# The v half of a spatial gating unit computed by token rows instead of by channels

## The chip, the core and the metric

The kernel runs on one core of a Trainium2 chip. The metric is device time in microseconds (us). All weights are read from device memory once per execution; activations stay in the core's on-chip memory (SBUF), and matrix products are accumulated in PSUM, which has eight banks of 512 fp32 columns in each of 128 partitions.

## What is computed

One step of an encoder layer for 320 token rows (256 of a prompt, 64 of running streams), width 2048. A normalised input is projected by `w_in`; its columns give queries, keys and values of a banded attention, and 1024 columns u and 1024 columns v of a spatial gating unit. Both mixers are normalised, concatenated, projected by `w_out`, and followed by an MLP of width 8192. What matters here is the gating:

```python
def rmsnorm(x, g):
    xf = x.astype(jnp.float32)
    y = xf * lax.rsqrt(jnp.mean(xf * xf, axis=-1, keepdims=True) + EPS)
    return (y * g.astype(jnp.float32)).astype(x.dtype)

def sgu_inputs(zs, g):
    a = jax.nn.gelu(zs)
    return a[..., :SGU_WIDTH], rmsnorm(a[..., SGU_WIDTH:], g)

def sgu_prompt(u, v, w_s, b_s):
    ...
    sp = jnp.einsum('gij,bnjgc->bnigc', ws, vb) + b_s.T[:, :, None]
    return u * sp.reshape(b, s, SGU_WIDTH)
```

So v is normalised over its 1024 channels, each of 8 channel groups is mixed over the tokens of a chunk by a matrix `ws`, and the result multiplies u. The normalised v rows of the 64 stream tokens are an output of their own (`sgu_v`).

## The kernel before, in words

**Products.** Activations are kept channels by tokens: `XH` and `XL` are 16 blocks of 128 channels by 320 tokens, the high and the low part of the normalised input, both in a reduced fp32 form (fp32r). A weight tile of 4 blocks by 256 columns (512 KB) is loaded by SP's DMA queue (`load`, line 94), split by ACT into `w_hi` (line 125) and by DVE into `w_lo` (line 126), and multiplied in three passes (line 136): `w_hi` with XH, `w_hi` with XL, `w_lo` with XH. The weights are the stationary operand (128 x 128), the activations stream as 320 columns. `products` does so for 256 output columns at a time, so one product is 16 blocks x 2 x 3 = 96 matmuls from 4 weight tiles. `w_hi` and `w_lo` have three buffers each.

**Order of the program.** First keys, values and the first quarter of the queries (line 196), with the input's loads interleaved; then the row norm of x (`rstd_rows`, line 154, and `spread`, line 165), three more products for the queries, four for v (lines 407 to 413), four for u (lines 439 to 456), 16 for `w_out`, then the MLP. Ten attention units (`attend`, line 321) are called ahead of the v products, four, three and three. A scheduler with its own timing model then decides the order of the instructions on each engine, so that attention, gating and products are interleaved; the order is fixed in the program and each engine runs it strictly.

**Scores.** A unit writes its scores by two matmuls into one PSUM tile `s_ps` of two banks (line 329), from which DVE reads four pieces (line 338); the tile has one buffer, so that the next unit's scores wait for these reads.

**The v half.** A product leaves v as 256 channels by 320 tokens. `gelu2` (line 395) scales by the row norm `rx`, and applies GELU on DVE, ACT and POOL. ACT squares and POOL adds for the norm of v (`add_square`, line 380), and POOL multiplies by the gain `g_sv` (line 413). After the fourth product the norm is taken (line 414: three small matmuls, DVE, and a power on POOL). Then 24 transposes on PE (line 422) bring v into token rows, and ACT copies them out of PSUM, scaled by the norm, into `vnat` and `vnat_s` (line 424). Eight groups follow: three matmuls with `wsT` into a bank `misc` (lines 430, 431), and DVE adds the bias `sgb` (lines 432, 435) to give `gv`, still by channels. The u products then multiply `gv` (line 453).

**After the gating.** `AH`, `AL` are the split attention output (`split`, line 175), `acc_a` the sum of its squares, added on POOL. `w_out`'s first half uses them, and its norm is `rstd_rows(acc_a)` and `spread` (line 465). Line 458 closes the pool `at`, which holds the attention's and the gating's tiles, `sgb` and `wsT` among them; the pool `wf` of the weight tiles of `w_out` and of the MLP takes its memory. So SP can issue the first load for `w_out` only when the last readers of `at` are done.

Of the kernel before, what the change touches and what calls it, by code (L numbers as in the profile page):

```python
# [8 lines left out]
F32 = mybir.dt.float32  # L9
F32R = mybir.dt.float32r  # L10
# [4 lines left out]
P = 128  # L15
T = 320
# [13 lines left out]
def hymba_step_kernel(ctx: ExitStack, tc: tile.TileContext, i, o):  # L30
# [13 lines left out]
    def misc():  # L44
        return ps_m.tile([P, 512], F32, name="misc", tag="misc")

# [59 lines left out]
    def products(w, k0, nk, jobs, rh, rl, first=None, deep=None):  # L106
# [4 lines left out]
        for a, n in chunks(nk, first is not None):  # L111
# [4 lines left out]
            for j, (c0, ps) in enumerate(jobs):  # L116
# [11 lines left out]
                tail = isinstance(ps, list) and a + n == nk  # L128
# [25 lines left out]
    def rstd_rows(sq, weight, eps, h=1):  # L154
# [6 lines left out]
        rs = sm.tile([P, 3 * h], F32, name="rs_rows", tag="rs_rows")  # L161
# [33 lines left out]
    q0_ps = ps_sc.tile([P, 2, 512], F32, name="q0_ps", tag="s_ps")  # L195
# [20 lines left out]
    nc.sync.dma_start(out=sinks, in_=i["sinks"])  # L216

# [35 lines left out]
    rx = spread(rstd_rows(ssq, inv_dm, EPS), "rx")  # L253
# [11 lines left out]
    def queries(g, q_ps):  # L265
        qg = qT[:, :, 2 * g:2 * g + 2]
        nc.vector.tensor_tensor(out=qg.rearrange("p b a t -> p a b t"),
                                in0=q_ps[:, :, 0:T].rearrange("p a (b t) -> p a b t", b=5),
                                in1=rx.rearrange("p (b t) -> p b t", b=5)[:, None].to_broadcast([P, 2, 5, 64]),
                                op=ALU.mult)  # L270
# [50 lines left out]
    def attend(unit):  # L321
# [4 lines left out]
        s_ps = ps_sc.tile([P, 2, 512], F32, name="s_ps", tag="s_ps")  # L326
        for j in range(2):
            a = 2 * (2 * kv + j)
            nc.tensor.matmul(out=s_ps[:, j, 0:2 * nk].rearrange("x (p k) -> x p k", p=2),  # L329
                             lhsT=qT[:, blk_, a:a + 2].rearrange("p a t -> p (a t)"),  # L330
                             rhs=kz[:, kv, :, k0:k0 + nk], start=True, stop=True)
# [3 lines left out]
        for p in range(2):  # L335
            for j in range(2):
                c = 2 * blk_ + p
                nc.vector.scalar_tensor_tensor(out=s[:, p, j, 0:nk], in0=s_ps[:, j, p * nk:(p + 1) * nk],
                                               scalar=rq[:, 2 * kv + j, c:c + 1],
                                               in1=bias[:, p, 2 * kv + j, b0:b0 + nk], op0=ALU.mult, op1=ALU.add)  # L340
# [64 lines left out]
    gv = blk("gv", [P, 8, T])  # L405
    acc_v = sums("acc_v")
    for g in range(4):
        attend_next((4, 3, 3, 0)[g])
        v_ps = product(w_in, 0, KT, 2304 + g * 256, xh, xl)
        gelu2(v_ps, gv[:, 2 * g:2 * g + 2])  # L410
        for a in range(2 * g, 2 * g + 2):
            add_square(acc_v, gv[:, a], a == 0)
            nc.gpsimd.tensor_scalar(out=gv[:, a], in0=gv[:, a], scalar1=g_sv[:, a:a + 1], scalar2=None, op0=ALU.mult)
    rv = rstd_rows(acc_v, inv_1k, 4 * EPS)
# [3 lines left out]
    for t, (t0, n) in enumerate(TT):  # L418
        for h in range(2):
            vps = misc()  # L420
            for a in range(4):
                nc.tensor.transpose(out=vps[0:n, a * P:(a + 1) * P], in_=gv[:, 4 * h + a, t0:t0 + n], identity=ident)  # L422
            dst = vnat[:, t] if t < 2 else vnat_s[0:HD]
            nc.scalar.activation(out=dst[:, h * 512:(h + 1) * 512], in_=vps[0:n], func=AF.Copy, scale=rv[0:n, t:t + 1])
    nc.gpsimd.dma_start(out=o["sgu_v"], in_=vnat_s[0:HD])
    for g in range(8):
        sp_ps = misc()
        cs = slice(g * P, (g + 1) * P)
        for b in range(2):
            nc.tensor.matmul(out=sp_ps[:, b * P:(b + 1) * P], lhsT=vnat[:, b, cs], rhs=wsT[:, g], start=True, stop=True)  # L430
        nc.tensor.matmul(out=sp_ps[:, 256:T], lhsT=vnat_s[:, cs], rhs=wsT[:, g, 0:HD], start=True, stop=True)  # L431
        nc.vector.tensor_tensor(out=gv[:, g, 0:256].rearrange("p (b i) -> p b i", b=2),
                                in0=sp_ps[:, 0:256].rearrange("p (b i) -> p b i", b=2),
                                in1=sgb[:, g, None, :].to_broadcast([P, 2, P]), op=ALU.add)
# [136 lines left out]
```

## Time and profile before

| | us |
|---|---|
| median of 3 runs (lowest, highest) | 1264.93 (1264.14, 1265.35) |
| the profiled execution | 1262.26 |
| its span, first to last instruction | 1259.7 |
| PE (TensorE) busy | 1252.3 |
| PE's weight loads busy | 1236.6 |
| DVE (VectorE) busy | 637.9 |
| ACT (ScalarE) busy | 489.4 |
| POOL (GpSimd) busy | 106.1 |

The profile is of one execution. A row of a group gives a line, an engine, the tiles written and read, the shape, the count, the busy time, the mean of one and the idle time ahead of them. A matmul's recorded duration overlaps that of its neighbours, so the time that a matmul costs is read from the chain of work that ended last, where a row gives a start, a length and a count of instructions in a row. An fp32 matmul is recorded as two instructions, an fp32r matmul or a transpose as one.

### The profile page before, as it was taken

What the parts mean: (1) busy time and instruction counts of PE and PEld (TensorE: products, weight loads), DVE (VectorE), ACT (ScalarE), POOL (GpSimd) and SP (SyncE); (2) the same over time, 40 slices, a digit from 0 to 9 for tenths busy, and PEclk for the clock granted to TensorE, in tenths of its full rate; (3) what the DMA queues carried; (4) which work ended last, traced back from release to release, by engine and by line L of the source; (5) the groups of instructions that cost most, each with busy time, mean ns of one, the idle gap of its engine ahead of it and who ended that gap; (6) DMA issues with size and microseconds to landing.
All of it is one profiled execution on the core that took longest, in us unless ns stands there. A gap on an engine that the chain in (4) does not pass through costs nothing.

```text
span 1259.7 us, 20182 instructions
## 1 busy us (share of the span) xinstructions
PE 1252.3 (99%) x8519; PEld 1236.6 (98%) x8519; DVE 637.9 (51%) x731; ACT 489.4 (39%) x636; POOL 106.1 (8%) x104
## 2 busy tenths in 40 slices
PE   8999999999999999999999999999999999999998
PEld 7998889999999999999999999999999999999998
DVE  7547857756864444444444444444444334444443
ACT  7335546533543342223333333343333333343221
POOL 2213452400310000000000000000000000000000
PEclk9999999999999999999999999999999999999999
DMA  8643233644454444445544444455444444444550
GB/s 281 191 136 116 85 109 119 216 148 137 151 149 148 152 149 149 149 147 150 150 150 151 150 151 151 151 151 151 150 151 150 146 148 149 148 153 160 169 169 32
DMA packets 186426, 187.77 MB, mean 149 GB/s; under 512 B 6464, under 2 KB 185856, under 8 KB 186336
## 3 DMA queue, kind: packets, MB, share of 16 engines
q1 hardware_dynamic: 185696, 185.43, 47.2%
q8 instruction: 66, 1.08, 0.4%
q0 software_dynamic: 496, 1.03, 0.3%
q14 instruction: 24, 0.20, 0.0%
q10 hardware_dynamic: 144, 0.03, 0.0%
HBM read 182.91 MB, written 3.32 MB: 148 GB/s over the span
## 4 chain that ended last, share of the span: by engine, by line
PE 98%; DMA 0%; SPq 0%; ACT 0%; issue 0%; DVE 0%
PE acc L136 93%; PE misc L136 1%; PE q_ps L136 1%; PE s_ps L329 1%; PE misc L374 1%; PE misc L365 1%; DMA xT<-in_xT 0%; SPq L99 0%; PE misc L275 0%; PE misc L430 0%; PE misc L158 0%; PE misc L422 0%; PE misc L169 0%; ACT XH L178 0%; PE misc L431 0%; ACT w_hi L125 0%
## 5 line engine op out<-in xcount | busy, mean ns | idle before, releaser
L126 DVE TENSOR_TENSOR w_lo<-w_raw,w_hi 128x1024 fp32r<-128x1024 f32 x332 | 413.6, 1246 | 460.6 <-ACT w_hi L125 451.2
L125 ACT ACTIVATE w_hi<-w_raw 128x1024 fp32r<-128x1024 f32 x332 | 351.9, 1060 | 708.0 <-PE acc L136 674.6
L136 PE MATMUL acc<-H2H,w_hi 128*128 128x320 f32 x1024 | 316.6, 309 | 0.0
L136 PE MATMUL acc<-H2L,w_hi 128*128 128x320 f32 x1024 | 316.4, 309 | 0.0
L136 PE MATMUL acc<-H2H,w_lo 128*128 128x320 f32 x1024 | 316.4, 309 | 0.0
L136 PE MATMUL acc<-FH,w_hi 128*128 128x320 f32 x992 | 306.5, 309 | 0.0
L136 PE MATMUL acc<-FL,w_hi 128*128 128x320 f32 x992 | 306.5, 309 | 0.0
L136 PE MATMUL acc<-FH,w_lo 128*128 128x320 f32 x992 | 306.5, 309 | 0.0
L136 PEld LDWEIGHTS acc<-H2L,w_hi 128*128 128x128 f32 x1024 | 192.2, 188 | 0.0
L136 PEld LDWEIGHTS acc<-H2H,w_hi 128*128 128x128 f32 x1024 | 192.2, 188 | 0.0
L136 PEld LDWEIGHTS acc<-H2H,w_lo 128*128 128x128 f32 x1024 | 192.2, 188 | 0.0
L136 PEld LDWEIGHTS acc<-FH,w_hi 128*128 128x128 f32 x992 | 186.2, 188 | 0.0
L136 PEld LDWEIGHTS acc<-FL,w_hi 128*128 128x128 f32 x992 | 186.2, 188 | 0.0
L136 PEld LDWEIGHTS acc<-FH,w_lo 128*128 128x128 f32 x992 | 186.2, 188 | 0.0
L136 PE MATMUL acc<-XH,w_hi 128*128 128x320 f32 x384 | 117.2, 316 | 1.2 <-ACT w_hi L125 1.1
L136 PE MATMUL acc<-XH,w_lo 128*128 128x320 f32 x384 | 116.8, 315 | 0.0
L136 PE MATMUL acc<-XL,w_hi 128*128 128x320 f32 x384 | 116.6, 314 | 0.0
L136 PEld LDWEIGHTS acc<-XH,w_hi 128*128 128x128 f32 x384 | 71.2, 189 | 4.7 <-ACT w_hi L125 2.2
L136 PEld LDWEIGHTS acc<-XL,w_hi 128*128 128x128 f32 x384 | 71.4, 189 | 2.4 <-issue 1.9
L136 PEld LDWEIGHTS acc<-XH,w_lo 128*128 128x128 f32 x384 | 71.1, 188 | 2.2 <-issue 1.5
L488 DVE SCALAR_TENSOR_TENSOR tf<-acc,r 128x640 f32<-128x640 f32 x32 | 26.4, 825 | 42.7 <-PE acc L136 42.7
L502 DVE TENSOR_TENSOR xT<-xT,acc 128x640 f32<-128x640 f32 x31 | 25.5, 821 | 41.8 <-PE acc L136 41.8
(176 smaller groups left out, 1016.9 us busy)
## 6 DMA issues: line engine op xcount, KB each, us to landing
w_raw<-in_w_up SPq DMA_DIRECT2D x128, 512.0 KB
w_raw<-in_w_down SPq DMA_DIRECT2D x128, 512.0 KB
w_raw<-in_w_in SPq DMA_DIRECT2D x44, 512.0 KB
w_raw<-in_w_out SPq DMA_DIRECT2D x32, 512.0 KB
w_first<-in_w_in SPq DMA_DIRECT2D x6, 512.0 KB
out_yT<-xT SPq DMA_DIRECT2D x7, 320.0 KB
xT<-in_xT SPq DMA_DIRECT2D x3, 640.0 KB
w_first<-in_w_in SPq DMA_DIRECT2D x8, 128.0 KB
```

The lines of the kernel that those rows point to most:

```text
L125: high = pin(nc.scalar.activation(out=hi[:, :n], in_=raw[:, :n], func=AF.Copy))
L126: low = pin(nc.vector.tensor_tensor(out=lo[:, :n], in0=raw[:, :n], in1=hi[:, :n].bitcast(F32), op=ALU.subtract))
L136: mm = nc.tensor.matmul(out=out, lhsT=w_[:, k, g * P:(g + 1) * P], rhs=r_(kk), start=(kk == 0 and x == 0), stop=(kk == nk - 1 and x == 2))
L329: nc.tensor.matmul(out=s_ps[:, j, 0:2 * nk].rearrange("x (p k) -> x p k", p=2), lhsT=qT[:, blk_, a:a + 2].rearrange("p a t -> p (a t)"), r ...
L365: nc.tensor.transpose(out=pt_ps[0:n, (2 * p + j) * P:(2 * p + j + 1) * P], in_=s[:, p, j, c:c + n], identity=ident)
L374: nc.tensor.matmul(out=o_ps[p * HD:(p + 1) * HD, 0:256], lhsT=v[0:n, kv], rhs=pt[0:n, p * 256:(p + 1) * 256], start=(x == 0), stop=(x == l ...
L488: nc.vector.scalar_tensor_tensor(out=t, in0=ps[:, :, 0:T], scalar=0.0, in1=r2[:, None, :].to_broadcast([P, 2, T]), op0=ALU.max, op1=ALU.mult)
L502: nc.vector.tensor_tensor(out=xT[:, a:a + n], in0=xT[:, a:a + n], in1=p, op=ALU.add)
```

## The change

For the v half the operands change places. Blocks of `XH` and `XL` with 128 tokens are stationary, and weight tiles of 2 blocks by 512 columns stream (`rows_product`). For each block there are three passes for each of the two prompt halves; for the 64 stream tokens a new tile `XS`, filled by POOL, holds XH and XL side by side as 128 stationary columns, so two passes (`w_hi`, `w_lo`) do. The two halves of its result are added afterwards through ACT and DVE (`low`). v so has two products of 16 x 8 = 128 matmuls of 512 columns, in place of four of 96 matmuls of 320 columns; the number of weight tiles, loads and splits is the same (16 of 512 KB).

v now lies in token rows. `gelu2_rows` takes the row norm of x as a scalar per partition (`rx_rows`, kept from `rstd_rows`), and ACT's last square also sums along the row (`acc_v`), so that the norm needs neither matmuls nor POOL's additions, and the 24 transposes go. ACT scales `vnat` and `vnat_s` in place. The gain moves behind the mixing (a scalar per channel in DVE's bias step); for the output `sgu_v` it is applied on POOL from a row copy of the gain, which a DMA writes at the start to device memory (`g_dram`, 1024 single values) and two DMAs read back later.

The v half needs a third PSUM bank for the stream rows, `v_s`. It takes one of the two banks of the scores: a unit's two score matmuls now use the single bank `s_ps` in turn, and the second waits for DVE's reads of the first. The first query product is written to these two banks separately. Attention units are called six and four ahead of the two products.

```diff
-    q0_ps = ps_sc.tile([P, 2, 512], F32, name="q0_ps", tag="s_ps")
+    q0_ps = [single("s_ps"), single("v_s")]
...
+    g_dram = dram.tile([8, P], F32, name="g_dram")
+    nc.gpsimd.dma_start(out=g_dram.rearrange("a p -> p a"), in_=g_sv)
...
-        s_ps = ps_sc.tile([P, 2, 512], F32, name="s_ps", tag="s_ps")
...
+        for j in range(2):
+            a = 2 * (2 * kv + j)
+            s_ps = single("s_ps")
+            nc.tensor.matmul(out=s_ps[:, 0:2 * nk].rearrange("x (p k) -> x p k", p=2),
+                             lhsT=qT[:, blk_, a:a + 2].rearrange("p a t -> p (a t)"),
+                             rhs=kz[:, kv, :, k0:k0 + nk], start=True, stop=True)
+            for p in range(2):
...
-    for g in range(4):
-        attend_next((4, 3, 3, 0)[g])
-        v_ps = product(w_in, 0, KT, 2304 + g * 256, xh, xl)
-        gelu2(v_ps, gv[:, 2 * g:2 * g + 2])
-        for a in range(2 * g, 2 * g + 2):
-            add_square(acc_v, gv[:, a], a == 0)
-            nc.gpsimd.tensor_scalar(out=gv[:, a], in0=gv[:, a], scalar1=g_sv[:, a:a + 1], scalar2=None, op0=ALU.mult)
-    rv = rstd_rows(acc_v, inv_1k, 4 * EPS)
...
+    XS = blk("XS", [P, KT, P], F32R)
+    nc.gpsimd.tensor_copy(out=XS[:, :, 0:HD], in_=XH[:, :, 256:T])
+    nc.gpsimd.tensor_copy(out=XS[:, :, HD:P], in_=XL[:, :, 256:T])
+
+    def rows_product(c0, ps, ps_s):
+        wv = w_in.rearrange("(kt p) n -> p kt n", p=P)
+        for a in range(0, KT, 2):
+            raw = wp.tile([P, 2, 512], F32, name="w_raw", tag="w_raw")
...
+            passes = [(t, k, x, w) for t in range(2) for k in range(2) for x, w in ((0, hi), (1, hi), (0, lo))]
+            passes += [(2, k, None, w) for k in range(2) for w in (hi, lo)]
...
+                st = XS[:, a + k] if t == 2 else (XH, XL)[x][:, a + k, t * P:(t + 1) * P]
...
+                nc.tensor.matmul(out=ps_s if t == 2 else ps[:, t], lhsT=st, rhs=w[:, k], start=(a == 0 and n == 1),
+                                 stop=(a == KT - 2 and n == (4 if t == 2 else 6)))
...
-            for a in range(4):
-                nc.tensor.transpose(out=vps[0:n, a * P:(a + 1) * P], in_=gv[:, 4 * h + a, t0:t0 + n], identity=ident)
...
+    for g in range(2):
+        attend_next((6, 4)[g])
+        cs = slice(g * 512, (g + 1) * 512)
+        v_ps, vs_ps = acc_tile(), single("v_s")
+        rows_product(2304 + g * 512, v_ps, vs_ps)
+        low = sm.tile([P, 512], F32, name="low", tag="w2", bufs=4)[0:HD]
+        nc.scalar.activation(out=low, in_=vs_ps[HD:P], func=AF.Copy)
+        nc.vector.tensor_tensor(out=low, in0=vs_ps[0:HD], in1=low, op=ALU.add)
...
+    for t in range(2):
+        nc.scalar.activation(out=vnat[:, t], in_=vnat[:, t], func=AF.Copy, scale=rv[:, t:t + 1])
+    nc.scalar.activation(out=vnat_s[0:HD], in_=vnat_s[0:HD], func=AF.Copy, scale=rv[0:HD, 2:3])
```

The scheduler orders the whole program anew. The place where this shows most is the passage from the u products to `w_out`. On PE before, from the last mixing matmuls of the gating (wsT) over the last u products (XH, XL) to the first products of `w_out` (AH, AL) and the norm sum of the attention (acc_a):

```order
L430 MATMUL misc<-wsT,vnat 128x128
L431 MATMUL misc<-wsT,vnat_s 128x64
L136 MATMUL acc<-XH,w_hi 128x320
...
L136 MATMUL acc<-XH,w_lo 128x320
L136 MATMUL acc<-AH,w_hi 128x320 [waits Activation_49]
L136 MATMUL acc<-AL,w_hi 128x320
L136 MATMUL acc<-AH,w_lo 128x320 [waits DVE_49]
...
L158 MATMUL misc<-inv_1k,acc_a 128x1 [waits Pool_49]
L158 MATMUL misc<-inv_1k,acc_a 128x1 x2
```

Here 138 u matmuls stand between the last mixing and the first AH, and 42 product matmuls between the norm's sums (line 158) and the matmuls that spread it (line 169). On PE now, at the same place:

```order
L490 MATMUL misc<-wsT,vnat_s 128x64
L139 MATMUL acc<-XL,w_hi 128x320
...
L139 MATMUL acc<-XH,w_lo 128x320
L161 MATMUL misc<-inv_1k,acc_a 128x1 [waits DVE_49,PE_49,Pool_49]
L161 MATMUL misc<-inv_1k,acc_a 128x1 x2
L139 MATMUL acc<-AH,w_hi 128x320 [waits Activation_49]
L139 MATMUL acc<-AL,w_hi 128x320
L172 MATMUL misc<-ident,rs_rows 128x128 [waits PE_49,Pool_49]
L172 MATMUL misc<-ident,rs_rows 128x128
L172 MATMUL misc<-ident,rs_rows 128x64
L139 MATMUL acc<-AH,w_lo 128x320 [waits DVE_49]
```

The last mixing matmuls have moved to 35 u matmuls ahead of the first AH, and two product matmuls are left between the norm's sums and the spread. On DVE before, from the last reader of `sgb` (gv<-misc,sgb) over the first `w_lo` of `w_out` (the row that also waits for DMASW3) to the norm's row r_rows:

```order
L432 TENSOR_TENSOR gv<-misc,sgb 128x256 [waits PE_49]
L435 TENSOR_TENSOR gv<-misc,sgb 128x64
...
L126 TENSOR_TENSOR w_lo<-w_raw,w_hi 128x1024 [waits DMASW3_49,DMAHW6_49,PE_49,Activation_49]
L179 SCALAR_TENSOR_TENSOR SL<-gv,cols,SH 128x320 [waits DVE_49,Activation_49]
L179 SCALAR_TENSOR_TENSOR SL<-gv,cols,SH 128x320 [waits Activation_49]
L126 TENSOR_TENSOR w_lo<-w_raw,w_hi 128x1024 [waits DMAHW7_49,PE_49,Activation_49]
L397 TENSOR_TENSOR z<-acc,rx 128x640 [waits PE_49]
L126 TENSOR_TENSOR w_lo<-w_raw,w_hi 128x1024 [waits DMAHW0_49,Activation_49]
L400 TENSOR_SCALAR gc<-gc 128x640 [waits Activation_49,Pool_49]
L160 TENSOR_SCALAR r_rows<-misc 128x3 [waits PE_49]
```

Three weight tiles of `w_out` are split ahead of r_rows. On DVE now, the same stretch:

```order
L415 SCALAR_TENSOR_TENSOR gu<-gc,z 128x640 [waits Activation_49]
L514 SCALAR_TENSOR_TENSOR gv<-gv,gu 128x640 [waits DVE_49]
L182 SCALAR_TENSOR_TENSOR SL<-gv,cols,SH 128x320 [waits PE_49]
L182 SCALAR_TENSOR_TENSOR SL<-gv,cols,SH 128x320 x2
L492 SCALAR_TENSOR_TENSOR gv<-misc,cols,sgb 128x256 [waits PE_49]
L495 SCALAR_TENSOR_TENSOR gv<-misc,cols,sgb 128x64
L182 SCALAR_TENSOR_TENSOR SL<-gv,cols,SH 128x320
L182 SCALAR_TENSOR_TENSOR SL<-gv,cols,SH 128x320 [waits DVE_49,Activation_49]
L182 SCALAR_TENSOR_TENSOR SL<-gv,cols,SH 128x320 [waits Activation_49]
L409 TENSOR_TENSOR z<-acc,rx 128x640 [waits PE_49]
L163 TENSOR_SCALAR r_rows<-misc 128x3 [waits PE_49]
L129 TENSOR_TENSOR w_lo<-w_raw,w_hi 128x1024 [waits DMAHW6_49,Activation_49]
```

The last reader of `sgb` (line 495) now stands four rows ahead of r_rows, and the first `w_lo` of `w_out` behind r_rows and behind z of the last u product.

More of the change, by code (lines that the diff above doesn't have):

```diff
@@ L334, in attend @@
             nc.gpsimd.memset(s[:, :, :, nk:P], 0.0)
-        for p in range(2):
-            for j in range(2):
+        for j in range(2):
[5 more added lines that the diff above has]
+            for p in range(2):
                 c = 2 * blk_ + p
-                nc.vector.scalar_tensor_tensor(out=s[:, p, j, 0:nk], in0=s_ps[:, j, p * nk:(p + 1) * nk],
+                nc.vector.scalar_tensor_tensor(out=s[:, p, j, 0:nk], in0=s_ps[:, p * nk:(p + 1) * nk],
                                                scalar=rq[:, 2 * kv + j, c:c + 1],
```

82 lines of the change are left out of this document (57 added, 25 removed).

## The prediction, on record before the run

> **What bounds the kernel now.** I read the page first, then the chain of work that ended last, then PE's waits and the groups of the other engines.
>
> ```profile
> span 1259.7 us, 20182 instructions
> PE 1252.3 (99%) x8519; PEld 1236.6 (98%) x8519; DVE 637.9 (51%) x731; ACT 489.4 (39%) x636; POOL 106.1 (8%) x104
> ```
>
> PE is busy for all but 7.4 us of the span; the profiled execution took 1262.26 us, 2.56 more than its span and 2.67 less than the median of 1264.93. I work out a difference to the profile and add it to the median. A measurement of this kernel can tell about 0.2%, 2.5 us, from no change.
>
> ```profile
> PE acc L136 <- ACT w_hi L125: 1.1, 1, 1.1
> 15.82 2.61 PE acc L136 x16
> 99.22 0.86 PE s_ps L329 x4
> 127.27 1.29 PE s_ps L329 x4
> 186.62 0.56 PE misc L158 x6
> 195.75 0.87 PE misc L422 x8
> 204.50 0.50 PE misc L430 x4
> 218.33 21.75 PE acc L136 x148
> 240.08 0.56 PE misc L158 x6
> 367.98 874.34 PE acc L136 x5961
> ```
>
> The first row, of PE's waits, is from the start of the program: later than that PE waits for nobody, the whole gating included. The others are rows of the chain (start, length, what). So two things count: how long PE's own instructions take, and whether the new order makes PE wait. A product matmul of 320 columns costs 874.34 / 5961 = 0.1467 us.
>
> **The matmuls of v.** Before: 384 x 0.1467 = 56.3 us. After: 256 matmuls of 512 columns, a size that the trace does not show. Its nearest rows are the fp32 score matmuls: 256 columns cost 0.86 / 4 = 0.215 us an instruction, 384 columns 1.29 / 4 = 0.3225, each instruction streaming its columns twice. The slope is 0.1075 / 256 = 0.00042 us per streamed column, and almost nothing is left at zero. At that slope 320 columns are 0.134 us, so an fp32r product carries 0.013 us on top. If this is fixed per matmul, 512 columns cost 0.215 + 0.013 = 0.228 us, or 58.3 us in all: 2.0 us more than before. If it vanishes for longer streams, 0.215 x 256 = 55.0, 1.3 less; if it grows with the columns, 0.1467 x 1.6 x 256 = 60.1, 3.8 more. I take the fixed case. Weight loading is not what makes it up: the norm's sums (line 158) stream one column and cost 0.56 / 6 = 0.093 us with their load, well below 0.1467.
>
> The Trainium skill, in "TensorE: Matmul & The Clock Gate", section "Back-to-back issue gap", gives a warm gap of columns / 2.4 + 2.5 ns. For 320 columns that is 136 ns, which the 147 ns of the trace contradict; for 512 it is 216 ns, an estimate by which v's matmuls would come to 55.2 us. That is the case of the vanishing extra, a rival below.
>
> ```profile
> L422 PE MATMUL misc<-ident,gv 128*128 128x128 f32 x16 | 2.4, 274 | 0.0
> L422 PE MATMUL misc<-ident,gv 128*64 128x128 f32 x8 | 1.2, 273 | 0.0
> ```
>
> **The transposes and the norm.** 24 transposes go, at 0.87 / 8 = 0.109 us: 2.6 us. The three sums of `acc_v` go, one 0.56 row. Both lie on PE, which has no idle time there: 3.2 us less. The mixing and the score matmuls stay the same in number.
>
> **Elementwise work.** POOL loses eight gains and seven additions and gets six products of 512 columns, two of the output's gain, the two `XS` copies and three more DMA issues.
>
> ```profile
> L401 POOL TENSOR_TENSOR gc<-gc,z 128x640 f32<-128x640 f32 x8 | 12.5, 1567 | 13.2 <-DVE gc L400 12.3 <-DVE nm L346 0.5 <-DVE r_rows L160 0.4
> L413 POOL TENSOR_SCALAR gv<-gv,cols 128x320 f32<-128x320 f32 x8 | 11.0, 1379 | 3.3 <-ACT acc_v L382 3.3
> L386 POOL TENSOR_TENSOR acc_v<-acc_v,sq 128x320 f32<-128x320 f32 x7 | 8.2, 1177 | 12.3 <-ACT sq L385 7.7 <-DVE den L356 4.6
> L126 DVE TENSOR_TENSOR w_lo<-w_raw,w_hi 128x1024 fp32r<-128x1024 f32 x88 | 114.6, 1303 | 64.9 <-ACT w_hi L125 63.0 <-PE misc L365 0.6
> L397 DVE TENSOR_TENSOR z<-acc,rx 128x640 f32<-128x640 f32 x8 | 6.5, 818 | 4.7 <-PE acc L136 4.7
> L399 ACT ACTIVATE gc<-z 128x640 f32<-128x640 f32 x8 | 5.8, 731 | 1.0 <-DVE z L397 0.9
> ```
>
> That is some 10 us less for POOL. GELU now runs over 6 x 512 columns instead of 4 x 640, a fifth more, and `low` is new: about 3 us more on DVE and on ACT (0.8 and 0.7 us per 640 columns).
>
> ```profile
> 120.00:140.00 20.00, 20.00 (x124) 16.68 (x123) 18.45 (x35) 10.68 (x28) 8.05 (x6) 1.00 0.36 107
> 200.00:220.00 20.00, 20.00 (x151) 20.00 (x150) 14.52 (x26) 11.56 (x21) 6.18 (x7) 1.00 0.39 119
> ```
>
> In these two stretches of the attention and the gating DVE (third time) is busy for 18.45 and 14.52 of 20 us, ACT (fourth) for 11 to 12, and PE is never idle; so I cost this at nothing. Without that cover it would be those 3 us. The second score matmul of a unit waits for two reads by DVE; the order puts some 20 instructions of PE, over 2 us, between the two, so I cost this at nothing too. What is queued behind that wait is the next product on PE, so a miss would cost PE directly.
>
> **The passage from u to `w_out`.** Here I expect a new wait. The split scores draw the attention out: its last output matmul now has 125 u matmuls behind it, where it had 319. The gating follows it, and only its last reader of `sgb` releases the memory in which `w_out`'s weights land.
>
> ```profile
> 221.53 0.21 DVE L435 TENSOR_TENSOR gv<-misc,sgb 128x64 f32<-128x64 f32 x1
> ...
> 221.90 1.47 SPq L99 DMA_DIRECT2D w_raw<-in_w_out  x3
> ...
> 33.12 0.44 SPq L99 DMA_DIRECT2D w_raw<-in_w_in  x1
> ...
> 37.12 1.06 ACT L125 ACTIVATE w_hi<-w_raw 128x1024 fp32r<-128x1024 f32 x1 [5.33 <-DMA w_raw<-in_w_in]
> ```
>
> The first two rows show this release: the last reader ends at 221.74, SP issues at 221.90, and u then runs to about 238.6, so 17 us cover the load. The last two show a load that ACT waited for: 4.0 us from issue to use, then 1.06 us on ACT. So the first `w_hi` comes some 5.2 us after the release.
>
> Now place the release. From the last attention output PE has 125 x 0.1467 = 18.3 us of u and eight mixing groups (0.50 for line 430, some 0.1 for line 431): 23 us. DVE has, by the order, from there to the last reader of `sgb`: three `w_lo` (3.9), eight bias steps (5.0), eight `AL` (4.3), three gv<-gv,gu (2.5), one each of z, gc, gu (2.4), three `SL` (1.6 to 3.2).
>
> ```profile
> L432 DVE TENSOR_TENSOR gv<-misc,sgb 128x256 f32<-128x256 f32 x8 | 3.3, 417 | 2.3 <-PE misc L431 2.2
> L435 DVE TENSOR_TENSOR gv<-misc,sgb 128x64 f32<-128x64 f32 x8 | 1.7, 211 | 0.0
> L179 DVE SCALAR_TENSOR_TENSOR AL<-ao,cols,AH 128x320 fp32r<-128x320 f32 x8 | 4.2, 542 | 0.0
> L179 DVE SCALAR_TENSOR_TENSOR SL<-gv,cols,SH 128x320 fp32r<-128x320 f32 x8 | 8.2, 1060 | 0.0
> L453 DVE SCALAR_TENSOR_TENSOR gv<-gv,gu 128x640 f32<-128x640 f32 x4 | 3.3, 822 | 0.1
> ```
>
> That is 19.7 to 21.3 us in a row, and it starts some 0.8 us after the last attention output; so the release comes 1 to 3 us before u ends (4 if some of it runs ahead), the first `w_hi` 1 to 4 us after it, and `w_lo`, 1.3 us, 2.5 to 5.5 us after.
>
> A second chain sets a floor. DVE runs z of the last product (0.82) and r_rows ahead of that `w_lo`, and only two product matmuls stand between the sums and the spread.
>
> ```profile
> 241.19 0.14 DVE L160 TENSOR_SCALAR r_rows<-misc 128x3 f32<-128x3 f32 x1
> 242.87 0.87 POOL L162 TENSOR_TENSOR rs_rows<-r_rows,nhalf 128x3 f32<-128x3 f32 x1
> ```
>
> From u's end: 0.2 to z, 0.82, 0.14, 0.1, 0.87, so the spread starts at 2.2 and ends at 2.8. Before, these steps lay under 42 matmuls. PE's own work there is 0.56 + 0.3 + 0.6 = 1.5 us. So PE idles 1.3 us at the least and 4 at the most. I take 2.6. POOL's last additions of `acc_a` (1.2 us each, as for `acc_v`) can hold the sums as well; by the same count they end within 1 us of u's end, inside this range.
>
> **The start.** `g_dram` is written by 1024 single values while the input loads fill the queues, and PE waits for them:
>
> ```profile
> 6.41 6.16 DMA xT<-in_xT
> 0.00:20.00 20.00, 15.93 (x82) 13.90 (x83) 11.89 (x31) 13.62 (x26) 6.08 (x18) 1.00 0.89 279
> q1 hardware_dynamic: 185696, 185.43, 47.2%
> ```
>
> A packet of this queue takes 0.472 x 16 x 1259.7 / 185696 = 0.051 us of an engine, nearly all of 1 KB. 1024 of them on 16 engines are 3.3 us, the upper bound; the lower is nothing, since 4 KB are 0.1% of what these 20 us move and 11% of the engines' time is free. I take 0.6, nearer to nothing. The Trainium skill, "DMA: Bandwidth & Descriptors", section "Rules for kernel authors", says that a strided last dimension becomes one descriptor per element, and so speaks against this write. No row here shows such a DMA; the full 3.3 us would add 2.7 to my sum.
>
> **Sum.** 2.0 - 3.2 + 2.6 + 0.6 = 2.0 us more. 1264.9 + 2.0 = 1266.9, that is 0.16% more, within what counts as the same.
>
> **The rivals.**
> *The extra of a product vanishes at 512 columns, and the new wait is at its floor* (0.19): -1.3 - 3.2 + 1.3 + 0.1 = -3.1, 1261.8. For it: weights are reloaded for every matmul, and a longer stream hides more of that. Against it: the 0.093 us with load.
> *The release comes late* (0.20): DVE's chain is at its slow end, with POOL beside it (`SL` took 1.06 us against 0.54 for the same shape in `AL`, `w_lo` 1.30 in the mean), or the attention ends later still. From the point where the release falls less than 2.5 us before u's end, every us late is one on the total. At 3 us later than in my sum: +5.0, 1269.9, slower. Against it: from 200 to 220 us DVE was idle for 5.5 of 20 us, and could run ahead.
> *The extra grows with the columns* (0.15): 3.8 - 3.2 + 2.6 + 0.6 = 3.8, 1268.7, slower. For it: 0.1467 is 1.1 times 0.134; against it: the fp32 rows show no such slope.
> *The forecast* has the rest, 0.46.
>
> **How the numbers follow.** The forecast's own terms move by about 1.5 either way; 0.08 of its 0.46 falls beyond +2.5 us and 0.05 below -2.5. Faster: 0.15 of the first rival, 0.05 here, 0.20. Slower: 0.20, 0.11 of the last rival, 0.08 here: 0.39. The same: 0.41. The range takes in the first rival's value and most of the late release, 1261.8 to 1271.0; what it leaves out is a release later than that, or the full 3.3 us at the start on top of a slow matmul.
>
> **What would show it.** The chain should show v's matmuls at 0.215, 0.228 or 0.235 us each. PE's waits should show one new wait of 1.3 to 4 us ahead of the spread or of the first `AH`, ended by POOL, ACT or DVE, with the first `w_out` load issued under 3 us before u ends. Then the start: the first long run of products began at 15.8 us and should begin up to 1 us later. I am wrong if PE idles within the v half or at the scores, which I cost at nothing, or if the load for `w_out` lands in time and PE does not wait at all; then the sum is -0.6 and the kernel stays the same or gets faster.

## The result, and the profile after

The changed kernel takes 1274.62 us (median of 4 runs, 1274.46 to 1275.65), the kernel before 1264.57 beside it (1264.14 to 1265.35): a ratio of 1.0081, 95% interval 1.0063 to 1.0098. It is slower by 10 us, and outside the predicted range of 1261.8 to 1271.0.

The first lines of the page of the changed kernel, and PE's waits in its trace (engine, tile and line, what was waited for: us in total, times, longest):

```profile
span 1272.7 us, 19881 instructions
...
PE 1256.1 (99%) x8361; PEld 1228.6 (97%) x8361; DVE 645.1 (51%) x741; ACT 491.7 (39%) x643; POOL 97.9 (8%) x99
```

```profile
PE acc L139 <- ACT w_hi L128: 8.5, 5, 4.7
PE s_ps L139 <- ACT w_hi L128: 2.5, 1, 2.5
...
PE misc L161 <- POOL acc_a L398: 0.8, 1, 0.8
```

The span grew by 13.0 us, PE's idle time from 7.4 to 16.6. The other 3.8 us are *busy* time, although the change takes work away from PE. Waits for weights are 11 us, where before they were 2.6. Rows of the chain that ended last (start, length, what) say where:

```profile
6.41 13.48 DMA xT<-in_xT
...
23.13 3.83 PE acc L139 x16
...
95.45 2.75 PE acc L439 x12
98.20 0.91 PE v_s L439 x4
...
240.39 1.38 DVE gv L514
...
244.63 1.06 POOL acc_a L398
245.69 3.46 DMA w_raw<-in_w_out
...
249.26 1.07 ACT w_hi L128
...
250.37 0.56 PE acc L139 x2
250.93 0.85 PE misc L172 x6
```

The input load that took 6.16 us before takes 13.48, and the first long run of products begins at 23.13, not at 15.82. v's matmuls of 512 columns cost 2.75 / 12 = 0.229 us. At the passage from u to `w_out` the first load is issued at 245.69, when u is already at its last matmul, and PE has the first `AH` product at 250.37.

The windows of both kernels add what the chain does not say. The columns are: stretch, length, busy time of PE, PEld, DVE, ACT, POOL; then the granted clock, the DMA share, GB/s. The changed kernel:

```profile
10.00:15.00 5.00, 1.64 (x12) 1.38 (x10) 0.89 (x2) 0.56 (x1) 0.00 (x0) 1.00 0.62 36
15.00:20.00 5.00, 1.97 (x6) 1.57 (x6) 0.43 (x1) 0.51 (x2) 0.00 (x0) 0.56 0.83 244
20.00:25.00 5.00, 3.83 (x13) 3.43 (x14) 4.16 (x7) 4.91 (x9) 0.00 (x0) 0.50 1.09 352
25.00:30.00 5.00, 5.00 (x33) 5.00 (x32) 4.86 (x9) 5.00 (x9) 0.00 (x0) 0.91 1.09 353
240.00:260.00 20.00, 16.50 (x105) 16.11 (x104) 16.96 (x22) 9.67 (x16) 12.21 (x11) 0.91 0.69 224
```

The same stretches before:

```profile
10.00:15.00 5.00, 3.15 (x20) 2.61 (x18) 2.05 (x6) 2.41 (x6) 0.00 (x0) 1.00 1.03 345
15.00:20.00 5.00, 4.18 (x28) 4.18 (x29) 4.56 (x6) 4.98 (x8) 0.00 (x0) 1.00 1.09 357
20.00:25.00 5.00, 5.00 (x34) 4.38 (x32) 5.00 (x9) 5.00 (x9) 0.00 (x0) 1.00 1.10 358
...
240.00:260.00 20.00, 20.00 (x141) 20.00 (x140) 14.22 (x17) 7.81 (x11) 5.12 (x5) 1.00 0.43 141
```

Two things are to be seen. From 10 to 15 us the input loads move 36 GB/s and not 345. And the granted clock, 1.00 everywhere before, falls to 0.50 after each of the two idle stretches: matmuls behind a wait run at half speed for some us. That is the busy time that the sum had no term for.

A table by stage makes this exact. Read from the starts of PE's product matmuls in the trace: *start* is up to the 101st product, *middle* from there to the last u product (queries, attention, v, mixing, u), *passage* from there to the 101st `w_out` product; the rest is within 0.1 us the same in both.

| us in the profile | start | middle | passage | span |
|---|---|---|---|---|
| before | 24.27 | 214.04 | 16.15 | 1259.7 |
| changed | 32.81 | 212.91 | 21.70 | 1272.7 |
| difference | +8.54 | -1.13 | +5.55 | +13.0 |

The spans differ by 13.0, the times of the two profiled executions by 12.2 (1274.46 and 1262.26) and the medians by 10.05: the profiled execution of before lies 2.3 us below its median and had one of the quick starts that are told of under the clock.

### The profile page after: what moved, and what is told of

Its sections match the earlier page's. It is cut to its first block, busy times and chain, and to the rows that moved or that the text cites. A ratio compares the mean times of both kernels' runs of the same rounds, so it can differ in the third digit from the quotient of the medians.

```text
span 1272.7 us, 19881 instructions
## 1 busy us (share of the span) xinstructions
PE 1256.1 (99%) x8361; PEld 1228.6 (97%) x8361; DVE 645.1 (51%) x741; ACT 491.7 (39%) x643; POOL 97.9 (8%) x99
## 3 DMA queue, kind: packets, MB, share of 16 engines
q8 instruction: 65, 1.06, 0.3%
## 4 chain that ended last, share of the span: by engine, by line
PE 97%; DMA 1%; DVE 1%; ACT 0%; SPq 0%; issue 0%; POOL 0%; ACTq 0%
PE acc L139 87%; PE acc L439 3%; PE v_s L439 1%; PE misc L139 1%; DMA xT<-in_xT 1%; PE s_ps L345 1%; PE misc L386 1%; PE misc L377 1%; PE s_ps L139 0%; PE v_s L139 0%; SPq L102 0%; PE misc L288 0%; DMA w_raw<-in_w_out 0%; PE misc L172 0%; ACT w_hi L128 0%; PE misc L489 0%
## 5 line engine op out<-in xcount | busy, mean ns | idle before, releaser
L129 DVE TENSOR_TENSOR w_lo<-w_raw,w_hi 128x1024 fp32r<-128x1024 f32 x316 | 394.7, 1249 | 447.3 <-ACT w_hi L128 438.5
L128 ACT ACTIVATE w_hi<-w_raw 128x1024 fp32r<-128x1024 f32 x316 | 334.8, 1060 | 686.6 <-PE acc L139 652.9
L139 PE MATMUL acc<-XH,w_hi 128*128 128x320 f32 x256 | 78.0, 322 | 5.9 <-ACT w_hi L128 5.9
L139 PE MATMUL acc<-XH,w_lo 128*128 128x320 f32 x256 | 77.6, 319 | 0.0
L139 PE MATMUL acc<-XL,w_hi 128*128 128x320 f32 x256 | 77.0, 317 | 0.0
L139 PEld LDWEIGHTS acc<-XH,w_hi 128*128 128x128 f32 x256 | 48.2, 194 | 9.0 <-ACT w_hi L128 7.9
L139 PEld LDWEIGHTS acc<-XL,w_hi 128*128 128x128 f32 x256 | 47.9, 192 | 2.1 <-issue 1.9
L139 PEld LDWEIGHTS acc<-XH,w_lo 128*128 128x128 f32 x256 | 47.4, 189 | 1.6 <-issue 0.8
```

The costliest lines, as they stand in the source:

```text
L128: high = pin(nc.scalar.activation(out=hi[:, :n], in_=raw[:, :n], func=AF.Copy))
L129: low = pin(nc.vector.tensor_tensor(out=lo[:, :n], in0=raw[:, :n], in1=hi[:, :n].bitcast(F32), op=ALU.subtract))
L139: mm = nc.tensor.matmul(out=out, lhsT=w_[:, k, g * P:(g + 1) * P], rhs=r_(kk), start=(kk == 0 and x == 0), stop=(kk == nk - 1 and x == 2))
```

## The experiments

Theory W: the write of the gain alone holds up the start. Theory P: the late release of the gating's memory makes the passage. Theory G: an idle stretch of PE costs more than itself, through the clock that is granted behind it. The rival V: the v half by rows costs the time. Each kernel is "before" or "changed" with one edit. Where the median of before is named, it is that of the same chip: 1264.4 to 1264.7.

**The write alone**, put into the kernel before (`b_write`), then as 128 pieces of 32 bytes (`b_write32`), then as 1024 pieces of 32 bytes (`b_write1k32`):

```diff
+    g_dram = dram.tile([8, P], F32, name="g_dram")
+    nc.gpsimd.dma_start(out=g_dram.rearrange("a p -> p a"), in_=g_sv)
```
```diff
+    g_dram = dram.tile([P, 8], F32, name="g_dram")
+    nc.gpsimd.dma_start(out=g_dram, in_=g_sv)
```
```diff
+    x_dram = dram.tile([8, P, 8], F32, name="x_dram")
+    nc.gpsimd.dma_start(out=x_dram.rearrange("a p r -> p a r"), in_=xT[:, 0, 0:64].rearrange("p (a r) -> p a r", a=8))
```

Expected of `b_write`: 

> The kernel before with only the write of the 1024 single gain values added, at the place where the changed kernel has it; nothing reads it. Theory W (the write alone holds up the input loads): 1264.6 + 8.5 = 1273 us (1272 to 1274.5), the first long run of products from about 23 us as in the changed kernel, not from 15.8. Rival V (the v half by rows, or the new order of the start, is what costs the time; the write only stands beside it): 1264 to 1266, the run from 15.8 to 16.8 us.

Expected of `b_write32`: 

> The kernel before with the same 4 KB written at the same place, but as 128 pieces of 32 bytes (the gain laid out by partition) instead of 1024 of 4 bytes. If the write costs by its pieces (W1): an eighth of 8.5, so 1265 to 1266. If any small write from this queue at this place holds up the loads (W2): about 1273 again. By rival V: 1264 to 1266, as for the first kernel.

Expected of `b_write1k32`: 

> The kernel before with 1024 pieces again at the same place, but of 32 bytes each (64 columns of the first input tile, eight at a time), 32 KB in all; nothing reads them. Theory N (the number of pieces holds up the loads): 1269 to 1271 us as with 1024 pieces of 4 bytes. Theory B (pieces of 4 bytes are what is dear, whatever their number): 1263 to 1265.5, as with 128 pieces of 32 bytes.

Measured: 1269.74 (ratio 1.0052, interval 1.0038 to 1.0067), 1262.70 (0.9991, 0.9981 to 1.0000) and 1261.97 (0.9987, 0.9978 to 0.9997). The row of each in the list of DMA issues (queue, number, KB, median us from issue to landing), in this order:

```profile
g_dram<-cols POOLq DMA_DIRECT2D x1, 4.0 KB, 10.1
```
```profile
g_dram<-cols POOLq DMA_DIRECT2D x1, 4.0 KB, 3.8
```
```profile
x_dram<-xT POOLq DMA_DIRECT2D x1, 32.0 KB, 4.2
```

All three are issued at 4.4 us. 1024 pieces of 32 bytes, eight times the data, land in 4.2 us, and the start is 24.51 us, against 24.27 before; 1024 pieces of 4 bytes take 10.1, and meanwhile the loads nearly stand. In the windows of `b_write`, which has no other change:

```profile
10.00:15.00 5.00, 3.44 (x14) 3.04 (x14) 0.85 (x2) 0.98 (x3) 0.00 (x0) 0.71 0.66 52
15.00:20.00 5.00, 2.37 (x7) 1.97 (x8) 1.62 (x4) 2.05 (x6) 0.00 (x0) 0.50 0.97 306
```

Its start is 32.08 us, middle and passage are those of before to 0.01 us. So theory W holds, and rival V falls for the start; not the number of pieces is dear, since as many of 32 bytes cost nothing. One rival is left untried: the 4-byte pieces also lie side by side in memory, eight of them in the 32 bytes that are one piece of `b_write1k32`, and 4-byte pieces far apart may cost less. My numbers for the median missed: I took 8.5 from the profiles, it is 5.4. The two 32-byte kernels came out 1.7 and 2.7 us *below* before, and below what I expected of them; the interval of the first touches 1, that of the second ends just under it. Part of it is the clock: four of the ten runs of each have a mean clock of 1.000, against 7 of 86 of before. Why their starts keep it more often is not shown.

**The changed kernel without the write**, the gain row read from an added input row of 1024 contiguous values (`a_input`), and with the same write later (`a_late`):

```diff
-    g_dram = dram.tile([8, P], F32, name="g_dram")
-    nc.gpsimd.dma_start(out=g_dram.rearrange("a p -> p a"), in_=g_sv)
...
-        nc.gpsimd.dma_start(out=sv, in_=g_dram.rearrange("a p -> (a p)")[None, g * 512:(g + 1) * 512]
-                            .to_broadcast([HD, 512]))
+        nc.gpsimd.dma_start(out=sv, in_=i["sgu_g"][:, g * 512:(g + 1) * 512].to_broadcast([HD, 512]))
```
```diff
-    g_dram = dram.tile([8, P], F32, name="g_dram")
-    nc.gpsimd.dma_start(out=g_dram.rearrange("a p -> p a"), in_=g_sv)
...
     for g in range(1, 4):
         queries(g, product(w_in, 0, KT, g * 256, xh, xl))
+    g_late = sm.tile([P, 8], F32, name="g_late", tag="g_late")
+    nc.vector.scalar_tensor_tensor(out=g_late, in0=rq[:, 2, 0:8], scalar=0.0, in1=g_sv, op0=ALU.mult, op1=ALU.add)
+    g_dram = dram.tile([8, P], F32, name="g_dram")
+    nc.gpsimd.dma_start(out=g_dram.rearrange("a p -> p a"), in_=g_late)
```

Expected of `a_input`: 

> The changed kernel, its gain row read from an input row of 1024 contiguous values, without the write. Theory W: 1274.6 - 8.5 = 1266 us (1265 to 1267), the first long run of products back at 15.8 us, and PE's idle 3.5 to 4 us at the passage from u to w_out still there. Rival V: 1273 to 1275.

Expected of `a_late`: 

> The changed kernel with the same 1024 single values written later, once the third group of queries is normed (at about 75 us), while the weight loads run up to three buffers ahead of PE. Theory W with the loads' lead as cover: the loads are held up again, but three buffers are some 10 us of products, so 1266 to 1268. If the lead is shorter than the hold-up: up to 1274, with a wait of PE for w_hi of some us behind the write. Rival V: 1273 to 1275 without such a wait.

Measured: 1268.79 (1.0037, 1.0024 to 1.0049) and 1270.07 (1.0048, 1.0031 to 1.0065). `a_late`'s write takes as long as ever, and its windows behind the write, the last two lines, show the loads slowed again:

```profile
g_dram<-g_late POOLq DMA_DIRECT2D x1, 4.0 KB, 10.2
...
85.00:90.00 5.00, 5.00 (x36) 5.00 (x35) 1.62 (x2) 1.06 (x1) 0.00 (x0) 1.00 0.25 25
90.00:95.00 5.00, 5.00 (x25) 4.18 (x24) 2.34 (x4) 1.75 (x2) 0.00 (x0) 1.00 0.50 39
```

But PE has no wait behind it, and the middle is 212.98 us against 212.91: three buffers of lead cover it. In the profiles its passage is 0.9 us longer than that of `a_input` (22.62 against 21.73; the clock stayed low for 6.8 us there instead of 3.4); whether that is its 1.3 us in the median is open, since the runs of `a_input` alone lie between 1265.17 and 1270.85. Both medians were forecast too low, for one reason: I took off the 8.5 us of the profiles for the write, and between the medians it is 5.8 (1274.62 less 1268.79). What is left over the kernel before is the passage. In the windows of `a_input`:

```profile
220.00:240.00 20.00, 17.54 (x128) 17.19 (x126) 18.93 (x28) 10.56 (x24) 16.19 (x14) 1.00 0.14 45
240.00:260.00 20.00, 18.94 (x119) 18.85 (x120) 15.46 (x17) 10.35 (x13) 5.07 (x4) 0.91 0.92 298
```

PE is idle for 2.46 + 1.06 = 3.5 us, and the second stretch loses 0.09 x 20 = 1.8 us to the clock. 1264.4 of before, less 1.1 in the middle, and 5.6 more in the passage are 1268.9, against the measured 1268.8; with runs that lie 5.7 us apart, so close an agreement is in part luck.

**The passage.** `a_wp` and the three below are `a_input` with a further edit. The first `w_out` product takes its weights through the pool of `w_in`'s, which waits for no release; in `a_wp2` the norm is also asked for behind that product; in `a_wp4` the first two products do so (without `a_wp2`'s edit), and `a_wp3` is that with the fill at the start that is told of below:

```diff
-            ps = product(i["w_out"], 8 * half, 8, g * 256, lambda k: hi[:, k], lambda k: lo[:, k], wf)
+            ps = product(i["w_out"], 8 * half, 8, g * 256, lambda k: hi[:, k], lambda k: lo[:, k],
+                         wf if half or g else None)          # a_wp4, a_wp3: wf if half or g > 1 else None
```
```diff
-        rm = spread(rstd_rows(acc, inv_1k, EPS), f"rm{half}")
         for g in range(8):
             ps = product(...)
+            if g == 0:
+                rm = spread(rstd_rows(acc, inv_1k, EPS), f"rm{half}")
```

Expected of `a_wp`: 

> The changed kernel without the write (gain row from an input), and the weights of the first w_out product land in the buffers of w_in, which need no release of the gating's memory. Theory P (that release makes the passage idle) with theory G (more than some 3 us of idle PE also halve the granted clock for the next us): PE idles under 1.5 us at the passage, the clock stays at 1.0 there, and the time is 1268.8 - 2.5 - 1.5 to 3 = 1263.5 to 1265 us. Rival S (the sums of acc_a on POOL and the spread set the passage, not the load): 1267.5 to 1269, PE idle still 3 us or more.

Expected of `a_wp2`: 

> The kernel with the first w_out product from the buffers of w_in, and the norm of the attention half asked for behind that product and not ahead of it. What PE still waits for there is 0.6 us for POOL's acc_a and 1.3 us for POOL's rs_rows; theory P with the floor of the prediction (the norm's chain): both go, 1265.7 - 1.9 = 1264 us (1263 to 1265). Rival: the waits move to the next product or to DVE, 1265 to 1266.5.

Expected of `a_wp3`: 

> The changed kernel without the write, the first two w_out products from the buffers of w_in, and the fill at the start (6 and 4 identity matmuls). With one product from there the chain of the norm (r_rows on DVE) still stood behind a w_lo that waited for the released memory; with two it should not: the passage costs 0.5 to 1 us over that of the kernel before, the middle is 1.1 shorter, the start 2.2: 1264.6 + 0.8 - 1.1 - 2.2 = 1262.1 us (1261.3 to 1263.3). Rival (POOL or DVE hold the norm up all the same): 1263.5 to 1265.

Expected of `a_wp4`: 

> The same without the fill at the start, so that the start is that of the kernel before: 1264.6 + 0.8 - 1.1 = 1264.3 us (1263.5 to 1265.5). Rival: 1265.5 to 1267.

| | us (median) | ratio to before | middle | passage |
|---|---|---|---|---|
| `a_input` | 1268.79 | 1.0037 (1.0024 to 1.0049) | 212.91 | 21.73 |
| `a_wp` | 1265.70 | 1.0003 (0.9993 to 1.0013) | 212.91 | 18.58 |
| `a_wp2` | 1266.38 | 1.0016 (1.0007 to 1.0026) | 212.92 | 19.40 |
| `a_wp4` | 1263.80 | 0.9995 (0.9985 to 1.0005) | 212.92 | 17.12 |
| `a_wp3` | 1262.06 | 0.9984 (0.9975 to 0.9993) | 212.91 | 17.12 |

In `a_wp2` the norm's sums of the second half of `w_out`, some 0.65 us, fall into the passage and are missing in the rest; beside the others its passage counts as 18.75.

`a_wp` shows theory P: without the wait for the release the passage is 3.15 us shorter, and the clock stays at 1.00 there. PE's idle time there, 1.9 us, and the median are a little above what I had forecast (under 1.5, and 1263.5 to 1265). What is left, in PE's waits:

```profile
PE misc L172 <- POOL rs_rows L165: 1.3, 1, 1.3
...
PE misc L161 <- POOL acc_a L396: 0.6, 1, 0.6
```

is the floor of the prediction, the norm's chain, and POOL's last addition ahead of it. What holds the norm up stands in the order of time of DVE (in brackets: idle before, and who ended it):

```profile
245.51 1.23 DVE L129 TENSOR_TENSOR w_lo<-w_raw,w_hi 128x1024 fp32r<-128x1024 f32 x1 [1.37 <-ACT w_hi L128]
246.65 0.15 DVE L163 TENSOR_SCALAR r_rows<-misc 128x3 f32<-128x3 f32 x1
```

`r_rows`, 0.15 us long, could run from 242, when its sums are done, and stands behind a `w_lo` whose weights do wait for the release. Asking for the norm later only moved this: in `a_wp2` the wait for `acc_a` is gone, but `r_rows` ran behind `gu` and `gv` of the last group, and the wait for `rs_rows` grew by as much. The edit was a miss.

```profile
PE misc L172 <- POOL rs_rows L165: 1.9, 1, 1.9
```

With two products clear of the release (`a_wp4`, `a_wp3`) the wait for `rs_rows` is gone, and of `a_wp3`'s passage this is left:

```profile
PE misc L165 <- POOL acc_a L400: 0.6, 1, 0.6
```

**The scores' one bank alone** (`b_one`): the kernel before with `single("s_ps")` per score matmul and the first queries in two single banks, as in the diff of the change.

Expected: 

> The kernel before with the scores, and the first queries, in single PSUM banks as in the changed kernel; v's half and all else as before. My forecast of nothing for this part: 1264.4 us, 1 either way, PE waiting nowhere in the scores; the attention ends later in the v half but u's 17 us still cover the load of w_out. Rival (the one bank holds up the attention so far that the passage gets late by itself): 1266 to 1270, with PE idle between u and w_out.

Measured: 1265.13 (1.0004, 0.9995 to 1.0013). Middle 214.12, passage 17.04: PE waits nowhere in the scores. The rows of the order give u products behind the last attention output: 319 before, 242 here, 125 in the changed kernel. So the bank draws the attention out, by some two thirds as far in matmuls of u as the rest of the change does; which part of that rest it is (the work on DVE and ACT, or the order of v's products) was not tried. 0.6 us of the 0.9 more in the passage are a wait for POOL's `acc_a`.

**The clock.** Identity matmuls that compute nothing used, put into a wait: at the passage of `a_input`, 28 (`a_warm`) and 11 (`a_warm2`); at the start of the kernel before, 10 and 4 ahead of the fifth tile's two products (`b_warm`), and 6 ahead of the fourth tile's second and 4 ahead of the fifth's first (`b_warm2`):

```diff
+    keep_ps = misc()
+    for _ in range(28):                                      # a_warm2: 11
+        with tc.issue_after(steps[-1][2]):
+            nc.tensor.matmul(out=keep_ps[:, 0:P], lhsT=ident, rhs=ident, start=True, stop=True)
```
```diff
                 load(raw[:, :n], wv[:, k0 + a:k0 + a + n, c0:c0 + 256])
+                if first is not None:
+                    for _ in range({(3, 1): 6, (4, 0): 4}.get((a, j), 0)):     # b_warm: {(4, 0): 10, (4, 1): 4}
+                        tc.keep_in_program_order(nc.tensor.matmul(out=warm_ps[:, 0:P], lhsT=ident, rhs=ident,
+                                                                  start=True, stop=True))
```

Expected of `a_warm`: 

> The changed kernel without the write, and 28 matmuls of the identity (about 0.11 us each, 3 us) in the idle stretch between u and w_out; they compute nothing that is used. The wait itself stays. Theory G: the granted clock stays at 1.0 over the passage and the products behind it run at full speed: 1268.8 - 1.5 to 3 = 1266 to 1267.3 us. Rival (the lower clock does not come from PE's idle stretch, or costs nothing): 1268.5 to 1269.5, the clock falling there as before.

Expected of `a_warm2`: 

> The changed kernel without the write, with 11 identity matmuls (2.45 us) between u and w_out, so that they fit into the wait of some 3.5 us and do not outlast it, as the 28 did (6.2 us). Theory G: the load still comes late, the clock stays at 1.0 there, 1268.8 - 1.5 to 3 = 1266 to 1267.3 us. Rival: 1268.5 to 1269.5, the clock falls at the passage all the same.

Expected of `b_warm`: 

> The kernel before with 14 matmuls of the identity (1.5 us in all) in the waits for the first input loads, 10 ahead of the fifth tile's first products and 4 ahead of its second. Theory G: the runs of before differ from 1261.6 to 1265.9 us with their mean granted clock (1.000 to 0.997), because in some of them the wait at the start is long enough to halve the clock; with the wait filled all runs have 0.999 to 1.000 and take 1261.5 to 1263.5. Rival (the clock has other causes): 1264.4 as before, or 1264.4 to 1266 if the fill delays products.

Expected of `b_warm2`: 

> The fill at the start again, where PE really waits: 6 identity matmuls ahead of the fourth tile's second products (idle there 0.9 to 2.9 us in five profiles) and 4 ahead of the fifth tile's first (0.3 to 1.1 us). Each is two passes of 0.11 us, 0.22 in all (the earlier fill was twice as long as meant, and stood behind the wait): 2.2 us. Theory G: the granted clock stays at 1.0 through the start in all runs, and they take 1261.5 to 1263.5 us, not 1264.5. Rival: 1264.5 to 1266.5, the clock falling all the same, or the fill and the order it brings costing what it saves.

`a_warm` took 1273.35 (1.0068, 1.0050 to 1.0085) and `b_warm` 1273.50 (1.0073, 1.0056 to 1.0090), and neither tested the theory. I had counted an fp32 matmul as one instruction of 0.11 us; it is recorded as two, so 28 were 6.2 us, longer than the wait. And `b_warm`'s stood behind the wait that they were to fill, which is that of the fourth tile, and changed the order of the queries' norms so that PE waited 4.4 us more between 46 and 55 us.

`b_warm2` fills the right wait: 1262.38 (0.9985, 0.9975 to 0.9994). Its windows:

```profile
10.00:15.00 5.00, 3.99 (x30) 3.77 (x29) 1.27 (x4) 1.87 (x5) 0.00 (x0) 1.00 1.06 351
15.00:20.00 5.00, 4.75 (x35) 4.56 (x34) 4.56 (x7) 5.00 (x8) 0.00 (x0) 1.00 1.09 355
```

and those of `b_one`, whose start has no fill and lost the clock:

```profile
10.00:15.00 5.00, 2.05 (x13) 1.79 (x12) 0.88 (x3) 1.26 (x4) 0.00 (x0) 0.94 1.01 349
15.00:20.00 5.00, 4.66 (x17) 4.26 (x17) 4.66 (x7) 5.00 (x9) 0.00 (x0) 0.50 1.09 355
```

17 matmuls against 35 in the same 5 us, with the loads at the same rate. All ten runs of `b_warm2` had a mean clock of 0.999 or 1.000, eight of them 1.000. Of 86 runs of the kernel before, the 7 at 1.000 have a median of 1262.1, the 32 at 0.999 of 1263.9, the 45 at 0.997 of 1265.2 (two more, at 0.998, lie between). That fits stretches of 3.4 us at half speed, the shortest in the traces: one loses 1.7 us and 0.14% of the mean clock, two lose twice that. Filling the wait at the start takes away most of this difference, and theory G holds there.

`a_warm2` took 1269.53 (1.0041, 1.0026 to 1.0056), no better than `a_input`. In its profile the fill kept the clock at the passage:

```profile
240.00:260.00 20.00, 18.05 (x129) 17.55 (x129) 16.30 (x22) 9.25 (x12) 8.82 (x8) 1.00 0.90 290
```

and the passage is 21.14 against 21.73 us; but its start lost the clock. It also has a wait of 0.7 us for DVE's `w_lo` that `a_input` has not. For the passage the theory is thus shown in the trace, with 0.6 us won there, and not in the time.

**All together** (`a_best`: `a_wp2` with the fill at the start).

Expected: 

> All together: the changed kernel without the write, the first w_out product from the buffers of w_in, the norm asked for behind it, and the fill at the start. If the terms add up: 1264 less 1 to 3 us of the clock at the start, 1261 to 1263, below both kernels. Rival: 1264 to 1266, no better than the kernel before.

Measured: 1265.92 (1.0006, 0.9996 to 1.0016): the rival. The fill kept the start (25.21 us), but the norm asked for late came with a wait of 2.65 us at the passage and the loss of the clock behind it (21.75, or 21.1 without the 0.65 from the rest). `a_wp3`, without that edit and with two products clear of the release, is the fastest with the v half by rows, 1262.06; `b_warm2`, without any of the change, takes 1262.38. Both lie some 0.15% below the kernel before; between these two the runs tell no difference.

## Why the prediction was wrong

**v's matmuls, transposes and norm: right.** Predicted +2.0 and -3.2, together -1.2; the middle is 1.06 to 1.13 shorter in every profile with the v half by rows (213.0 or 212.9 against 214.04). A product matmul of 512 columns costs 0.229 us, forecast 0.228: the extra is fixed per matmul. The rivals of a vanishing and of a growing extra are out. By the formula that the Trainium skill, "TensorE: Matmul & The Clock Gate", section "Back-to-back issue gap", gives for an isolated matmul, it would have been an estimated 216 ns; the 229 ns of the trace contradict that for this stream.

**Elementwise work and the scores' bank: right.** Both were costed at nothing, and PE waits nowhere in the middle.

**The start: the failed step.** The sum had 0.6 us, with 3.3 as the upper bound, from a packet of SP's queue at 0.051 us. That price is of a load of 1 KB from memory, and I took it as an upper bound for a *write* of 4 bytes because a smaller packet should not cost more. The row was of another kind in two ways, direction and size, and the price of packets is not where the cost lies: the trace of `b_write` holds the write as 16 packets of 256 bytes that end by 7.9 us, and the loads slump behind them, from 244 GB/s between 7 and 8 us to 85, 60 and 67 in the three after. The write lands after 10 us, and the loads beside it fall to about a tenth of their rate. With the clock, it is 8.5 us between the profiles and 5.4 in the medians. The rule of the Trainium skill that the prediction weighed ("DMA: Bandwidth & Descriptors", section "Rules for kernel authors": one descriptor per element) spoke against the write; I kept the row's price.

**The passage: right mechanism, too small.** The new wait is there, at the place named. The release came 0.3 us before u's end, where I had 1 to 3, so the rival of the late release was nearer. DVE's chain to it ran with hardly a pause from 223.04 to 245.61, 22.6 us where I had 19.7 to 21.3, and some of its instructions took far longer than their like before, as this one of the changed kernel, 0.54 us in the mean of before:

```profile
236.26 1.84 DVE L182 SCALAR_TENSOR_TENSOR AL<-ao,cols,AH 128x320 fp32r<-128x320 f32 x1
```

That POOL, at work beside it, slowed it, as the rival had it, is not shown. The idle time is 3.5 us, in my bounds of 1.3 to 4, where I took 2.6. What no term held is the clock: 0.50 for 3.4 us behind the wait, an estimated 1.7 us more. That is 5.2 of the 5.55; the last 0.35 is not placed.

**The sum.** Without the write term, 1264.4 - 1.1 + 5.6 = 1268.9 against 1268.8 measured; with it, 1268.9 + 5.4 = 1274.3 against 1274.6. The terms account for the whole, though the passage's 5.6 is from profiles and the write's 5.4 from medians. The prediction fell by two: 0.6 for 5.4, and 2.6 for 5.6.

## What to carry to other kernels

Price a wait of the engine that sets the end by its length *and* by what the granted clock does behind it: here 2.7 us of idle brought 3.4 us at half speed, up to 1.7 us more, and the profile's clock column, read in windows, shows it. Never take a row of another direction and size as an upper bound for a transfer; four-byte pieces written to memory beside critical loads are to be moved, as in `a_late`, or made 32 bytes long, as in `b_write1k32`. And look at where the profiled execution lies among the runs: its start may be the lucky one.

## What the runs showed of the hardware that I had not expected

- 1024 writes of 4 bytes took 10.1 to 10.9 us to land and, issued from another engine's queue than the loads, brought what all queues move from 345 to 36 GB/s; 1024 of 32 bytes took 4.2 us and cost nothing that could be measured. The Trainium skill, "DMA: Bandwidth & Descriptors", section "Specifications", says that transfers under 512 B are read, modified and written. If that is what made the 4-byte pieces dear, it did not make the 32-byte pieces so; no run here shows the mechanism.
- The granted clock fell to 0.50 after idle stretches of 2.7 us (four profiles at the passage) and once after 1.8 us, and not after 0.6, 1.3, in `a_wp2` 1.9 or, at the start of `b_write1k32`, 2.9. The length of one wait does not decide it. In the 17 traces, up to the last product, every stretch between two changes of the clock is a multiple of 3.41 us (3.41, 6.83, 10.24, 13.65 and so on); cut into windows of that length, PE's idle time *summed* over a window goes with the clock of the next. At full clock none of the windows with up to 1.6 us idle was followed by 0.50, all 14 with 1.85 us or more were, and two of five between 1.67 and 1.78. At half clock the 16 with 0.34 us idle or less were followed by 1.00, the 12 with 0.62 or more were not. First `b_write1k32`, where a wait of 2.9 us falls on two windows, then `a_wp`, where waits of 2.2 and 1.1 us do (length, then PE's busy time; the clock is third from the end):

```profile
10.87:14.29 3.42, 2.33 (x16) 2.06 (x15) 1.16 (x3) 1.74 (x4) 0.00 (x0) 1.00 1.08 359
14.29:17.70 3.41, 1.64 (x11) 1.64 (x12) 2.80 (x5) 3.11 (x5) 0.00 (x0) 1.00 1.09 353
17.70:21.11 3.41, 3.41 (x25) 3.41 (x24) 3.27 (x5) 3.41 (x8) 0.00 (x0) 1.00 1.08 356
...
9.69:13.11 3.42, 2.06 (x15) 1.80 (x13) 0.56 (x2) 0.09 (x1) 0.00 (x0) 1.00 1.04 350
13.11:16.52 3.41, 1.45 (x8) 1.16 (x9) 2.57 (x6) 3.41 (x7) 0.00 (x0) 1.00 1.06 364
16.52:19.93 3.41, 3.41 (x14) 3.41 (x14) 3.31 (x4) 3.41 (x6) 0.00 (x0) 0.50 1.09 354
```

  The Trainium skill, "TensorE: Matmul & The Clock Gate", section "What's actually happening", has windows of 3.4 us that run freely, a halved clock after an idle one and the full clock after a busy one. The lengths agree, and so does that waits of the same length go either way, by where they fall; but a window need not be wholly idle: in these traces about half was enough.
- An fp32 matmul of 128 columns takes two recorded instructions of 0.111 us, 0.22 in all (56 in 6.2 us in `a_warm`), not the 0.109 of a transpose of the same size.
